# Layer one of a hybrid decoder: input products by seven quarter sums, with the recurrence fed from DRAM

## The chip, the cores and the metric

One core of a Trainium2 chip runs the whole program. The metric is the device time of one execution in microseconds (us), and the change is judged by the median of several executions of the kernel before and after it. The engines are PE (TensorE: matmuls and transposes), DVE (VectorE), ACT (ScalarE), POOL (GpSimd) and SP, the queue from which every DMA of this kernel is issued.

## The reference

The program is a decoder trunk of two layers over x of 1024 tokens by 1024 features. Layer one is a gated linear recurrence (HGRN2) with 16 heads of 128; layer two is forgetting attention (FoX) with keys and values of its own. The change is in layer one:

```python
q, fz, i, g = jnp.split(h @ w_in, 4, axis=-1)      # h: 1024 x 1024, w_in: 1024 x 8192
logf = jnp.log(lb + (1.0 - lb) * jax.nn.sigmoid(fz))
k = (1.0 - lb) * jax.nn.sigmoid(-fz)
...
b = jnp.cumsum(logf, axis=3)                        # within chunks of 64 tokens
q_dec, k_in, k_st = q * jnp.exp(b), k * jnp.exp(-b), k * jnp.exp(b_last - b)
att = jnp.where(causal, jnp.einsum('bhnck,bhnsk->bhncs', q_dec, k_in), 0.0)
...                                                 # state = dl * state + k_st^T v, o = q_dec state + att v
o = _rms(o, onorm_g.reshape(A_HEADS, HEAD_DIM))
return (o * jax.nn.silu(g)) @ w_out
```

## The kernel before

Every large product is made in three passes: each operand is split into a high part that the PE takes fast and a low remainder (`halves`: a copy on ACT, then a subtraction on POOL or DVE), and high*high, high*low and low*high are summed in PSUM. The activations h, transposed and split, stay in SBUF.

Layer one works through eight pairs of heads (`hg_pair`). A pair takes four weight matrices of 1024 by 256 columns, here called v, g, f and q after what they make (value, gate, forget, query). g, f and q are made transposed (`gemm_T`, head dimension in the partitions, 512 tokens in a row: 24 matmuls of 512 columns for a head and token half); v is made with tokens in the partitions (`gemm_N`, 192 matmuls of 256 columns). One such matrix is the unit of time of this document; a pair is four of them.

Around the products runs the recurrence, for both heads of a pair and one half of the tokens at a time (`hg_half`). Its pieces for one head and half are: `hg_forget` (three sigmoid and logarithm passes on ACT, a scan and a chain of small operations on DVE, four exponentials on ACT, products on DVE; each switch between sigmoid, logarithm and exponential loads a table), `hg_att` (8 matmuls, a masked copy on DVE, 4 transposes), `hg_state` (up to 4 matmuls and a chain of DVE steps), `hg_out` (8 matmuls, then a square on ACT and on DVE the reduction L542, the helper `rsqrt_mean` with 12 operations of 128x4, and the product L544) and `hg_turn` (4 transposes, a scaled copy on ACT, a product with the gate on POOL, stores to DRAM). Beside these, three column pairs of the condition's projections are summed on DVE in every pair (`mod_sum`, L268 and L271: eight operations for each).

The order on PE is fixed while the program is written: a class `Weave` chains all PE instructions, and the pieces of the recurrence are generators that are advanced after so many microseconds of product work (`yield 4.5` and the like). The order on DVE, ACT, POOL and SP is the scheduler's. Each engine works its own list strictly in that order.

## Time and profile before

| | us |
|---|---|
| median of 3 runs (2373.2 to 2376.35) | 2374.51 |
| the profiled execution, own time | 2370.9 |
| its span, first to last instruction | 2369.2 |
| one pair in the steady part (158.9 to 271.8) | 112.9 |
| PE busy in it | 109.3 |
| DVE, ACT, POOL busy in it | 66.9, 49.4, 27.0 |

The profile is of one execution. The second group of the table is read from a stretch that holds one pair exactly; PE's busy time counts matmuls that overlap in its pipeline, so what matters is where it stands idle and how far apart equal instructions start.

### The profile page before, as it was taken

To read this page: it belongs to the slowest core of one execution; us is meant where nothing else is said; L and a number is where in the kernel's file an instruction comes from. 1 tells how busy PE (TensorE), PEld (TensorE's weight loads), DVE (VectorE), ACT (ScalarE), POOL (GpSimd) and SP (SyncE) were. 2 spreads that over 40 slices of the span, in tenths; PEclk is the share of its full clock that TensorE was granted. 3 is DMA by queue.
4 is the path that set the end of the run, shared out by engine and by line. 5 is a ranking of instruction groups with operands and counts; after the bars stand their busy time and mean duration, and the time that the engine had idled before them with its cause. 6 is when DMAs were issued, how large, how long until landed. Compare 5 with 4: busy or idle time off the path is not lost.

```text
span 2369.2 us, 38021 instructions
## 1 busy us (share of the span) xinstructions
PE 2263.2 (96%) x14376; PEld 2026.4 (86%) x14376; DVE 1501.3 (63%) x3838; ACT 1016.6 (43%) x1634; POOL 601.9 (25%) x514
## 2 busy tenths in 40 slices
PE   4999999999999999999798999999999999999999
PEld 3888888888888798788688999989999999998887
DVE  7565555665656566646867547667767766777533
ACT  5454444444353536324323324444544544455321
POOL 3222222221222221101332222433343334333000
PEclk9999999999999999999899999999999999999999
DMA  8313131313132223565322323512222222235443
GB/s 272 102 41 103 45 98 46 98 54 98 55 89 72 72 85 95 189 217 182 106 90 81 124 86 99 177 57 68 88 74 73 88 78 84 68 94 175 154 145 115
DMA packets 220315, 245.18 MB, mean 103 GB/s; under 512 B 14610, under 2 KB 182964, under 8 KB 220132
## 3 DMA queue, kind: packets, MB, share of 16 engines
q1 hardware_dynamic: 220132, 242.75, 32.8%
q8 instruction: 113, 1.85, 0.3%
q14 instruction: 70, 0.57, 0.1%
HBM read 196.36 MB, written 46.34 MB: 102 GB/s over the span
## 4 chain that ended last, share of the span: by engine, by line
PE 73%; DVE 11%; ACT 6%; issue 4%; DMA 4%; POOL 1%; SPq 0%; ACTq 0%; DVEq 0%; POOLq 0%
PE mm L48 53%; PE oa L48 8%; PE sm L48 7%; PE sm L51 5%; DVE blk L233 2%; DVE blk L271 1%; DVE dl L479 1%; ACT blk L232 1%; DVE blk L473 1%; ACT L472 1%; DMA blk<-in_mod_w_dram 1%; ACT L487 1%; ACT blk L472 1%; POOL blk L233 1%; ACT L470 1%
## 5 line engine op out<-in xcount | busy, mean ns | idle before, releaser
L48 PE MATMUL mm<-blk,blk 128*128 128x512 f32 (+1 forms) x9120 | 1726.0, 343 | 15.2 <-DVE blk L233 7.9
L48 PEld LDWEIGHTS mm<-blk,blk 128*128 128x128 f32 x9120 | 1419.5, 192 | 185.9 <-DVE blk L233 10.5
L232 ACT ACTIVATE blk<-blk 128x1024 fp32r<-128x1024 f32 (+3 forms) x372 | 335.4, 914 | 461.2 <-PE mm L48 281.1
L233 DVE TENSOR_TENSOR blk<-blk,blk 128x1024 fp32r<-128x1024 f32 (+3 forms) x268 | 276.2, 1039 | 228.8 <-ACT blk L232 225.2
L233 POOL TENSOR_TENSOR blk<-blk,blk 128x1024 fp32r<-128x1024 f32 (+1 forms) x104 | 240.0, 2314 | 308.6 <-ACT blk L232 302.5
L48 PE MATMUL oa<-blk,blk 128*128 128x256 f32 (+1 forms) x2016 | 286.4, 287 | 27.8 <-DVE blk L523 14.7
L48 PEld LDWEIGHTS oa<-blk,blk 128*128 128x128 f32 x2016 | 267.4, 196 | 39.2 <-DVE blk L523 16.0
L48 PE MATMUL sm<-blk,blk 128*128 128x256 f32 (+6 forms) x1824 | 269.2, 303 | 0.1
L48 PEld LDWEIGHTS sm<-blk,blk 128*128 128x128 f32 (+2 forms) x1824 | 218.2, 175 | 23.2 <-issue 3.5
L51 PE MATMUL sm<-ident,blk 128*128 128x128 f32 x1201 | 187.8, 277 | 36.2 <-DVE blk L931 12.6
L51 PEld LDWEIGHTS sm<-ident,blk 128*128 128x128 f32 x1201 | 144.6, 142 | 63.3 <-issue 32.0
L1226 ACT ACTIVATE blk<-blk,m 128x128 f32<-128x128 f32 (+7 forms) x128 | 99.0, 773 | 127.5 <-DVE m L1224 117.4
L233 DVE TENSOR_TENSOR blk<-sm,blk 128x512 fp32r<-128x512 f32 (+1 forms) x160 | 92.9, 581 | 62.7 <-ACT blk L232 62.2
L1228 POOL TENSOR_SCALAR blk<-blk,smx 128x128 f32<-128x128 f32 (+7 forms) x128 | 98.1, 767 | 135.6 <-DVE smx L1227 121.2
L271 DVE SCALAR_TENSOR_TENSOR blk<-blk,cc,blk 128x256 f32<-128x256 f32 x196 | 111.2, 570 | 20.6 <-DMA blk<-in_mod_w_dram 13.8
L1198 POOL TENSOR_TENSOR blk<-rows4k,keep 128x128 f32<-128x128 f32 x128 | 63.0, 492 | 226.8 <-DVE mx L1205 208.4
L553 POOL TENSOR_TENSOR blk<-blk,blk 128x512 f32<-128x512 f32 x32 | 42.5, 1327 | 238.4 <-ACT blk L552 238.4
L232 ACT ACTIVATE blk<-sm 128x512 fp32r<-128x512 f32 (+1 forms) x160 | 81.1, 507 | 48.7 <-PE sm L51 47.9
L1205 DVE CUSTOM_DVE_ANT_0 blk<-sm,rows4k 128x128 f32<-128x128 f32 (+3 forms) x176 | 84.6, 494 | 22.9 <-PE sm L48 21.4
L474 POOL TENSOR_SCALAR blk<-blk,cc 128x512 f32<-128x512 f32 x32 | 22.9, 716 | 260.7 <-ACT blk L471 257.4
L487 ACT ACT_TABLE_LOAD x31 | 39.8, 1283 | 103.0 <-DVE blk L482 103.0
L473 DVE TENSOR_TENSOR_SCAN blk<-rows4k,blk 128x512 f32<-128x512 f32 x32 | 39.1, 1223 | 70.3 <-ACT blk L472 70.3
(167 smaller groups left out, 1776.2 us busy)
## 6 DMA issues: line engine op xcount, KB each, us to landing
blk<-in_a_w_in_dram SPq DMA_DIRECT2D x64, 512.0 KB, 3.9
blk<-in_mod_w_dram SPq DMA_DIRECT2D x48, 512.0 KB, 4.7
blk<-in_kv_w_dram SPq DMA_DIRECT2D x32, 512.0 KB, 4.1
blk<-in_b_w_in_dram SPq DMA_DIRECT2D x32, 512.0 KB, 3.9
ogd<-blk SPq DMA_DIRECT2D x128, 64.0 KB, 1.9
blk<-in_kv_mod_w_dram SPq DMA_DIRECT2D x16, 512.0 KB, 3.5
blk<-in_a_w_out_dram SPq DMA_DIRECT2D x16, 512.0 KB, 3.9
blk<-ogd SPq DMA_DIRECT2D x16, 512.0 KB, 3.8
```

What stands on the lines that cost most here:

```text
L48: self._chain(self.PE.matmul(*a, **k))
L51: self._chain(self.PE.transpose(*a, **k))
L232: S.activation(hi, src, AF.Copy)
L233: eng.tensor_tensor(lo, src, hi.bitcast(F32), ALU.subtract)
L271: V.scalar_tensor_tensor(acc, rawk(rb, k), csil[:, k:k + 1], acc, ALU.mult, ALU.add)
L472: S.activation(u["lf"], u["lf"], AF.Ln, bias=lc, scale=oc)
L473: V.tensor_tensor_scan(u["b"], rst, u["lf"], 0.0, ALU.mult, ALU.add)
L487: S.activation(lf[:, :, 1, :], lf[:, :, 1, :], AF.Exp)
L1198: G.tensor_tensor(nfm, nF[:, i * P:n], negm, ALU.add)
L1205: V.tensor_tensor_reduce(dst, src, add, 1.0, -3e38, ALU.add, ALU.max, mx[:, nm:nm + 1])
L1226: S.activation(l[:, 0:n], l[:, 0:n], AF.Exp, bias=m, accum_out=sm)
L1228: G.tensor_scalar(l[:, 0:n], l[:, 0:n], sm, 0.0, ALU.mult, ALU.add)
```

## The change

From the second kind of the first pair on, each weight matrix (29 of 32; v, f and q of the first pair stay as they were) is multiplied by the scheme of seven products of quarters: activations and weights are cut in two along both the contraction and the other dimension, seven sums or differences of quarters are made on each side, seven products of 512 x 128 x 512 are made instead of eight, and the four quarters of the result are put together from them. The seven operands of the activations are made once (`sums`). Those of the weights are made matrix by matrix (`sa_prep`): four sums and differences on POOL, seven splits with the low part on POOL for five of them and on DVE for two. A product of a quarter is 12 matmuls of 512 columns; `sa_step` names them m = 1, 6, 2, 7, 5, 4, 3, in this order, in three PSUM banks. A result is read by ACT or added up by DVE (L747 to L757) and stored to DRAM, 256 KB for a head and token half.

The recurrence becomes a thread for each head and token half (`hg_thread`), four a pair, started after 19.0 units of product work each (the program counts 28 ticks of 0.68 for a matrix). A thread loads its f, q and v from DRAM, and g later; v arrives transposed and is turned with 4 transposes more (`hg_values`). Two threads have a set of buffers each; a third waits for the turn of the first. The condition's sums are now one for each matrix, for the first 24 matrices.

```diff
-    def hg_half(p, th, v, sg):
-        for j in range(2):
-            hg_att(j)
-            PE.marks.add(("att", p, j, th))
-            yield 4.5
...
-        for j in range(2):
-            hg_out(2 * p + j, j, th, v)
-            PE.marks.add(("out", p, j, th))
-            yield 5.0
-        yield 2.0
-        for j in range(2):
-            hg_turn(2 * p + j, j, th, sg)
-            yield 3.0
...
+    def hg_thread(p, i):
...
+        if i >= 2 or p > 0:
+            yield from PE.wait(("turn", *((p, i - 2) if i >= 2 else (p - 1, i + 2))))
+        hg_load(p, i)
+        yield 3.5
+        if not first:
+            yield from PE.wait(("gate", *before))
+        hg_forget(p, i, None if first else 1 - j)
+        PE.marks.add(("forget", p, i))
+        yield 10.0
+        hg_att(j)
+        yield 3.0
+        hg_values(j)
+        yield from PE.wait(("mat", "g", p, i))
+        dma(us[j]["g"], hgd["g", p, i])
+        PE.marks.add(("gate", p, i))
+        yield 2.5
+        hg_state(j, th)
+        yield 5.0
+        hg_out(j, th)
+        yield 6.0
+        if not last:
+            yield from PE.wait(("forget", *((p, i + 1) if i < 3 else (p + 1, 0))))
+        hg_turn(p, i)
+        PE.marks.add(("turn", p, i))
+        yield 0.0
...
+    def hg_spawn(p):
+        for i in range(4):
+            PE.spawn(hg_thread(p, i), (2.0 + 19.0 * i) if p + 1 < NP else (2.0, 15.0, 33.0, 46.0)[i])
...
+        b11, b12, b21, b22 = B(0, 0), B(0, 1), B(1, 0), B(1, 1)
+        if m == 6:
+            G.tensor_tensor(b12, b22, b12, ALU.subtract)
+            G.tensor_tensor(b11, b11, b12, ALU.add)
+        if m == 7:
+            G.tensor_tensor(b21, b21, b11, ALU.subtract)
+        if m == 5:
+            G.tensor_tensor(b11, b22, b11, ALU.subtract)
+        halves(V if m in (6, 5) else G, *sa_slot(i), {1: b11, 6: b11, 2: b21, 7: b12, 5: b11, 4: b21, 3: b22}[m])
...
+        for k in range(4):
+            ah, al = [c512(full(m, k // 2, lo).bitcast(F32R))[:, k % 2, :] for lo in range(2)]
+            for y, (lh, rh) in enumerate(((wh, ah), (wh, al), (wl, ah))):
+                PE.matmul(ps, lhsT=lh[:, k, :], rhs=rh, start=first and k == 0 and y == 0,
+                          stop=last and k == 3 and y == 2, skip_group_check=True)
+            PE.tick(0.68)
...
+        if xi == 5 and n < len(mods_left):
+            acc = accs[n % 2]
+            mod_sum((raw_next(), acc))
+            PE.spawn(mod_later(mods_left[n], acc), 8.0)
+        sa_prep(i + 2)
+        sa_step(i)
```

On POOL, in the steady part of layer one, a whole pair of the kernel before stands in these rows and the few before them: splits of weights 1024 wide (L233), the scale of k (L474), the product with the gate (L553).

```order
L474 TENSOR_SCALAR blk_1_106<-blk_1_106,cc 128x512
L233 TENSOR_TENSOR blk_1_88<-blk_1_96,blk_1_86 128x1024
L233 TENSOR_TENSOR blk_0_91<-blk_0_93,blk_0_89 128x1024
L233 TENSOR_TENSOR blk_1_92<-blk_1_94,blk_1_90 128x1024
L553 TENSOR_TENSOR blk_0_117<-blk_0_117,blk_0_99 128x512
L553 TENSOR_TENSOR blk_0_117<-blk_0_117,blk_1_100 128x512
```

In the kernel after, the following rows are less than one matrix of the four. L237 are low parts (of the operands m = 2, 7, 4, 3 and of the next matrix's 1), L727, L724, L729 and L725 the sums of weight quarters, L508 the scale of k, L597 the product with the gate.

```order
L237 TENSOR_TENSOR blk_1_1034<-blk_1_106,blk_1_1034 128x512
L727 TENSOR_TENSOR blk_1_106<-blk_1_106,blk_0_105 128x4x128
L724 TENSOR_TENSOR blk_0_93<-blk_1_94,blk_0_93 128x4x128
L729 TENSOR_TENSOR blk_0_105<-blk_1_106,blk_0_105 128x4x128
L508 TENSOR_SCALAR blk_0_813<-blk_0_813,cc 128x512
L237 TENSOR_TENSOR blk_0_1035<-blk_0_105,blk_0_1035 128x512
L237 TENSOR_TENSOR blk_1_1034<-blk_1_106,blk_1_1034 128x512
L237 TENSOR_TENSOR blk_0_1035<-blk_1_106,blk_0_1035 128x512
L597 TENSOR_TENSOR blk_0_817<-blk_0_817,blk_1_820 128x512
L237 TENSOR_TENSOR blk_0_1033<-blk_0_95,blk_0_1033 128x512
L725 TENSOR_TENSOR blk_0_95<-blk_0_95 128x4x128
```

What moved: between the low parts of m = 2 and m = 7 stand three sums and the scale of k in one run, and there are 12 POOL operations a matrix where there were four.

On DVE, the normalisation of one thread's result stands behind the forget chain of the next. Before, the rows from the last products of a forget chain (L489, L488, L490) to the reduction of a result (L542) are these, with state steps (L525, L520) and the product with q (L633) between them.

```order
L489 TENSOR_TENSOR blk_1_110<-blk_1_106,blk_0_105 128x4x64
L525 SCALAR_TENSOR_TENSOR blk_1_116<-blk_1_116,dl,sm 128x128 x2
L633 TENSOR_TENSOR blk_0_111<-mm,blk_1_108 128x512
L525 SCALAR_TENSOR_TENSOR blk_1_116<-blk_1_116,dl,sm 128x128
L488 TENSOR_TENSOR blk_0_109<-blk_0_109,blk_1_106 128x512
L520 TENSOR_SCALAR blk_1_116<-blk_1_116,dl 128x128
L490 TENSOR_TENSOR blk_1_110<-blk_0_109,dl 128x4x64
L542 TENSOR_REDUCE ss<-blk_1_112 128x4
```

After, L749 adds up the result of m = 6, L523, L522 and L525 are the products of the forget chain, L237 is the low part of the operand of m = 5, L582 the reduction, and the rows of 128x4 behind it the start of `rsqrt_mean`.

```order
L749 TENSOR_TENSOR blk_0_115<-mm,blk_0_115 128x512
L561 TENSOR_SCALAR blk_0_821<-blk_0_821,dl 128x128
L523 TENSOR_TENSOR blk_1_818<-blk_1_818,blk_0_817 128x512
L522 TENSOR_TENSOR blk_0_819<-blk_0_819,blk_1_818 128x512
L525 TENSOR_TENSOR blk_0_819<-blk_1_818,dl 128x4x64
L237 TENSOR_TENSOR blk_0_1035<-blk_0_93,blk_0_1035 128x512
L582 TENSOR_REDUCE ss<-blk_1_814 128x4
L225 TENSOR_SCALAR rs_m<-ss 128x4
L226 TENSOR_SCALAR rs_t<-rs_m 128x4
L227 TENSOR_SCALAR rs_y<-rs_t 128x4
```

What moved: the low part of a PE operand is now in this list, and in every matrix the normalisation of a result, for which PE waits, begins behind the whole forget chain of another head.

On PE, the transposes of `hg_turn` (L51, x4) wait for that normalisation. Before, 33 matmuls of 512 columns stand between the last of `hg_out` and the first turn, whose end is this:

```order
L48 MATMUL mm<-blk_0_73,blk_1_90 128x512
L48 MATMUL mm<-blk_1_74,blk_1_90 128x512
L48 MATMUL mm<-blk_0_73,blk_1_92 128x512
L51 MATMUL sm<-ident,blk_1_112 128x128 x4
L48 MATMUL mm<-blk_0_75,blk_1_90 128x512
L48 MATMUL mm<-blk_1_76,blk_1_90 128x512
```

After, the turn stands in the last quarter of the step m = 5 (its weights are in block 1035), and 24 matmuls lie between `hg_out` and it; the row behind the three that follow begins m = 4.

```order
L48 MATMUL mm<-blk_1_826,blk_0_1035 128x512
L48 MATMUL mm<-blk_0_825,blk_0_1035 128x512
L51 MATMUL sm<-ident,blk_1_814 128x128 x4
L48 MATMUL mm<-blk_0_825,blk_0_1035 128x512
L48 MATMUL mm<-blk_1_826,blk_0_1035 128x512
L48 MATMUL mm<-blk_0_825,blk_0_1035 128x512
L48 MATMUL mm<-blk_0_89,blk_0_1033 128x512
```

What moved: the turn comes after fewer matmuls, and what follows it (m = 4, `hg_att`, m = 3, `hg_values`) is queued behind it.

## Rows read from the trace of the kernel before

**Rows 1.** Windows of one pair: window, length, busy us (count) by engine, clock, DMA.

```profile
158.90:271.80 112.90, 109.33 (x673) 95.45 (x672) 66.92 (x157) 49.37 (x68) 26.96 (x17) 0.98 0.25 75
```

**Rows 2.** Chain that ended last: first products of pairs 1 and 7 (start, us, what).

```profile
158.94 5.74 PE mm L48 x48
...
838.14 5.74 PE mm L48 x48
```

**Rows 3.** The same chain within a pair, 271 to 385 us.

```profile
279.18 4.31 PE mm L48 x36
...
288.77 0.44 PE sm L51 x4
...
317.72 25.19 PE mm L48 x111
...
348.14 5.50 PE mm L48 x24
...
354.56 1.02 PE sm L48 x12
...
376.88 6.18 PE mm L48 x24
```

**Rows 4.** Groups by shape, 264 to 377 us: count, busy us, mean ns, idle before.

```profile
L233 POOL TENSOR_TENSOR blk<-blk,blk 128x1024 fp32r<-128x1024 f32 x8 | 19.0, 2380 | 27.4 <-ACT blk L232 27.4
...
L271 DVE SCALAR_TENSOR_TENSOR blk<-blk,cc,blk 128x256 f32<-128x256 f32 x21 | 11.6, 552 | 1.3 <-DMA blk<-in_kv_mod_w_dram 0.9
...
L553 POOL TENSOR_TENSOR blk<-blk,blk 128x512 f32<-128x512 f32 x4 | 5.5, 1370 | 25.7 <-ACT blk L552 25.7
```

**Rows 5.** Timeline of DVE (start, us): small operations, alone and beside POOL.

```profile
301.85 2.38 DVE L227 SCALAR_TENSOR_TENSOR rs_y<-rs_t,rs_y 128x4 f32<-128x4 f32 x1
...
336.94 0.17 DVE L479 COPY dl<-blk 128x4 f32<-128x4 f32 x1
...
360.70 2.19 DVE L479 COPY dl<-blk 128x4 f32<-128x4 f32 x1
```

**Rows 6.** Timeline of POOL at the same places.

```profile
301.82 4.72 POOL L233 TENSOR_TENSOR blk<-blk,blk 128x1024 fp32r<-128x1024 f32 x2 [10.52 <-ACT blk L232]
...
360.50 2.36 POOL L233 TENSOR_TENSOR blk<-blk,blk 128x1024 fp32r<-128x1024 f32 x1 [2.42 <-ACT blk L232]
```

**Rows 7.** Timeline of ACT in one forget chain.

```profile
332.06 0.60 ACT L470 ACTIVATE blk<-mm 128x512 f32<-128x512 f32 x1 [4.12 <-PE mm L48]
...
334.46 0.82 ACT L472 ACTIVATE blk<-blk,cc 128x512 f32<-128x512 f32 x1
337.78 1.28 ACT L487 ACT_TABLE_LOAD   x1 [2.50 <-DVE blk L482]
...
340.02 0.61 ACT L486 ACTIVATE blk<-blk 128x512 f32<-128x512 f32 x1
```

**Rows 8.** Timeline of DVE in the same chain.

```profile
335.69 1.22 DVE L473 TENSOR_TENSOR_SCAN blk<-rows4k,blk 128x512 f32<-128x512 f32 x1
...
337.27 0.42 DVE L482 TENSOR_TENSOR blk<-dl,blk 128x256 f32<-128x256 f32 x1
...
340.66 0.69 DVE L488 TENSOR_TENSOR blk<-blk,blk 128x512 f32<-128x512 f32 x1 [0.64 <-ACT blk L486]
341.39 0.42 DVE L490 TENSOR_TENSOR blk<-blk,dl 128x256 f32<-128x256 f32 x1
```

**Rows 9.** Timeline of DVE: two normalisations, first and last operation of each.

```profile
276.50 0.68 DVE L542 TENSOR_REDUCE ss<-blk 128x4 f32<-128x512 f32 x1
...
279.60 0.69 DVE L544 TENSOR_TENSOR blk<-oa,rs_y 128x512 f32<-128x512 f32 x1
...
308.51 0.68 DVE L542 TENSOR_REDUCE ss<-blk 128x4 f32<-128x512 f32 x1
...
313.97 0.68 DVE L544 TENSOR_TENSOR blk<-oa,rs_y 128x512 f32<-128x512 f32 x1
```

**Rows 10.** DMA issues: KB each, median us from issue to landing.

```profile
vd<-blk SPq DMA_DIRECT2D x32, 256.0 KB, 2.9
```

More of the change, by code (lines that the diff above doesn't have):

```diff
@@ L60, in _step, with wait @@
             self.threads.remove(th)
+    def wait(self, mark):
+        while mark not in self.marks:
+            yield 0.5
     def tick(self, us):
@@ L186, in hybrid_trunk_kernel @@
     V.memset(st1, 0.0)
-    xt = [ar(14 + t // 2, (t % 2) * 1024, 1024) for t in range(NT)]
+    xt = [ar(t // 2, (t % 2) * 1024, 1024) for t in range(NT)]
     def load_x(*ts):
@@ new lines, in hg_thread @@
+    def hg_thread(p, i):
+        j, th = i % 2, i // 2
+        first, last = (p, i) == (0, 0), (p, i) == (NP - 1, 3)
+        before = (p, i - 1) if i else (p - 1, 3)
+        if i >= 2 or p > 0:
[23 more added lines that the diff above has]
+        yield 0.0
@@ L641, in mod_later, with put, early @@
         yield 0.0
-    for p in range(NP):
-        wv, wg = hg_pair(p, wv, wg)
+    stage = [ar(20, 0, 512), ar(20, 512, 512), ar(24, 1024, 512), ar(24, 1536, 512)]
+    def put(kind, p, i, ps, to, eng=S):
+        if eng is S:
+            S.activation(to, ps, AF.Copy)
+        else:
+            V.tensor_copy(to, ps)
+        dma(hgd[kind, p, i], to)
+    def early(kind, w, i, to):
+        ps = mm_ps()
+        gemm_T(ps, w, i % 2, i // 2)
+        put(kind, 0, i, ps, to, V if i % 2 else S)
@@ new lines, in hybrid_trunk_kernel, with full, sums, whole @@
+    renew(16, 17)
+    wv = split_a((16, 17))
+    for i in range(4):
+        put("f", 0, i, fps[i], stage[i], V if i % 2 else S)
+    for i in range(2):
+        put("q", 0, i, qps[i], us[i]["b"], V if i % 2 else S)
+    for i in (2, 3):
+        early("q", wq, i, us[i - 2]["ks"])
+    for j in range(2):
+        G.memset(us[j]["att"], 0.0)
+    def full(m, kk, lo, n=1024):
+        return pr(AOPS0[m][kk], 1024 * lo, n)
+    def sums(kk):
+        x, y, w = [pr(b, 1024 * kk, 1024) for b in (19, 23, 18)]
+        z = (pr(20, 0, 1024), pr(24, 1024, 1024))[kk]
+        def whole(eng, dst, m):
+            eng.tensor_tensor(dst, full(m, kk, 0), full(m, kk, 1), ALU.add)
+        whole(G, y, 4)
+        whole(V, z, 1)
+        whole(V, x, 3)
+        whole(G, w, 2)
+        V.tensor_tensor(y, y, x, ALU.add)
+        V.tensor_tensor(x, z, x, ALU.subtract)
+        V.tensor_tensor(z, y, z, ALU.subtract)
+        V.tensor_tensor(w, w, z, ALU.subtract)
+        def split(m, src):
+            halves(V, full(m, kk, 0).bitcast(F32R), full(m, kk, 1).bitcast(F32R), src)
+        split(7, x)
+        split(6, z)
+        return [lambda: split(5, y), lambda: split(3, w)]
@@ new lines, in hybrid_trunk_kernel @@
+    rst = ar(24, 1536, 512)
+    G.memset(rst, 1.0)
+    G.memset(c64(rst)[:, :, 0:1], 0.0)
+    renew(19, (20, (0,)))
+    hg_spawn(0)
+    sa_prep(0)
+    sa_prep(1)
+    for part in later:
+        part()
+    for i, (n, m) in enumerate(SSTEPS):
+        xi = i - 7 * n
+        if xi == 0:
+            for _ in range(2 if n < len(mods_left) else 1):
+                raw_load()
+        if xi == 5 and n < len(mods_left):
[4 more added lines that the diff above has]
+        sa_step(i)
+        if xi == 6 and MATS[n][0] == "q":
+            hg_spawn(MATS[n][1])
@@ L647, in gate_rows @@
+    hblk[:] = range(8)
     def gate_rows(l, gt, row):
@@ L823, in a_ready @@
     def a_ready(t):
-        PE.need(("half", NP - 1, t // 4))
+        for j in range(2):
+            PE.need(("turn", NP - 1, 2 * (t // 4) + j), fair=True)
     def a_row(t, ch):
```

243 lines of the change are left out of this document (124 added, 119 removed).

## The prediction

> **What bounds the kernel now.** First the windows of one pair of layer one [rows 1]: PE is busy for 109.3 of 112.9 us, DVE for 66.9, POOL for 27.0. So PE sets the time here, with 3.6 us of idle. Then the chain that ended last: the first products of pair 1 and pair 7 start at 158.94 and 838.14 us [rows 2], so a pair takes (838.14 - 158.94) / 6 = 113.2 us, and a matrix, a quarter of it, **28.3 us**. That is the figure against which the change has to be set. The chain within a pair [rows 3] is PE nearly throughout: 111 matmuls of 512 columns take 25.19 us, 0.227 each; 36 of 256 columns take 4.31, 0.120 each; four transposes 0.44. Last, who makes PE wait: the groups of POOL [rows 4] and the timelines of DVE and POOL side by side [rows 5, 6]. A copy of 128x4 on DVE takes 0.17 us at 336.94 and 2.19 at 360.70; in between nothing differs but a POOL subtraction that runs from 360.50 to 362.86, and the copy ends 0.03 us behind it. A rsqrt step at 301.85 takes 2.38 us beside the first of two such subtractions. These operations of DVE do not run beside a POOL operation; they end with it.
>
> **What the products save.** A matrix falls from 96 matmuls of 512 columns to 84: 12 x 0.227 = 2.7 us. The v matrix, 192 x 0.120 = 23.0 us before, was 1.2 us more than 96 x 0.227 = 21.8, or 0.3 a matrix; v's transposes in every thread cost 0.44. PE's work of a matrix was 109.3 / 4 = 27.3, and becomes 27.3 - 2.7 - 0.3 + 0.4 = **24.7 us**. If PE were never kept waiting, 28 matrices would give back 28 x 3.6 = 101 us. So the question is what else becomes the bound.
>
> **What the other engines get.** POOL had 27.0 / 4 = 6.7 us a matrix. Now it has five low parts, four sums, two gate products, each of 512 elements, and the scale of k: the 1024-wide one takes 2.38, the 512-wide ones up to 1.37, a lone one about 1.3 [rows 4], so 11 x 1.3 plus at most 1.3 makes about 15.0. DVE had 16.7 and gets two low parts, five additions of results and, for 24 matrices, one condition sum where it had three quarters of one; it loses the product that made the gate. That is about 6 us more, 22 to 23 of 28.3. Neither is full by itself, but DVE works its list in order, waits for POOL operation by operation, and PE waits for DVE in each matrix: for the low part of the operand of m = 5, then for the normalised result that `hg_turn` transposes.
>
> **The loop that sets a matrix.** I follow one matrix from the end of `hg_values` to the same point in the next; each leg is queued behind the one before it.
>
> - ACT to the logarithm. The copy of v and one high part lie ahead (0.5 each by the spacing of the ACT rows), then two sigmoids, the table and the logarithm: 332.06 to 335.28 is 3.2 us [rows 7]. Together 4.2.
> - DVE, scan to the subtraction for which the exponentials wait: 335.69 to 337.69, 2.0 us when POOL is idle [rows 8]. But here POOL has the low part for m = 2, three sums, the scale of k and the low part for m = 7 in one run, six operations, some 7.4 us that begin with the ACT leg. The scan gets in between two of them (1.2 us) and each small copy behind it waits for the next, as in rows 5; so the subtraction ends about 7.4 + 1.2 + 0.7 = 9.3 us after the start of the loop, not 6.2. I take 9.3 for the two legs.
> - ACT, table and four exponentials: 337.78 to 340.63, 2.9 us [rows 7].
> - DVE: the product with q (0.6), the two k products (340.66 to 341.81, 1.15 [rows 8]), the low part for m = 5 (0.6), and one low part of POOL (m = 4) in their way, 1.3: 3.6. Alone 2.3; with two operations in the way 4.9.
> - DVE, normalisation: 276.50 to 280.29, 3.8 us alone, 308.51 to 314.65, 6.1 us with a condition sum's pieces in between [rows 9]. In three orders of four the list after has such pieces there, and POOL's low part for m = 3 falls into it. I take 5.0 for the 24 matrices with a condition sum and 4.2 for the others.
> - PE, from the turn to the end of `hg_values`: 0.4, three matmuls of m = 5 (0.7), m = 4 (2.7), `hg_att` with its transposes (1.5), m = 3 (2.7), 0.4: 8.4 us [rows 3].
>
> The sum is 9.3 + 2.9 + 3.6 + 5.0 + 8.4 = 29.2, and some 0.1 us at each of five hand-overs: **29.7 us** with a condition sum, **28.9** without. PE's own work of 24.7 lies inside it: PE would stand idle for about 5 us of each matrix, most of it in m = 5 and at the turn, since only 24 matmuls (5.5 us) cover the way from `hg_out` to the turn.
>
> **The sum.** 24 x (29.7 - 28.3) = 33.6 and 4 x (28.9 - 28.3) = 2.4. The first pair: before, 2.5 matrices of 21.8 us after the start-up, 54.5; after, six products of 24 matmuls (32.7) and one matrix in seven parts (19.1), 51.8, behind which the quarter sums of the activations must come in time: taken as even. The last threads run into the output projection, as the last half pair did, but two of them are started after the last matrix: +4, between 0 and 10. Results of 256 KB go to DRAM and come back: a store like it lands in 2.9 us [rows 10], a load takes no less, and the slices lie a matrix ahead of their reading except v's and g's of the first thread, which lie some 10 us ahead. I cost this at nothing; cover gone, it is the third rival. Added to the profiled execution's own 2370.9 this makes 2410.9; the runs' median lies 3.6 above that execution, so the forecast in their terms is **2414 us**.
>
> **A rule of the skill.** The rows show DVE operations with two operands in SBUF, and a copy, ending together with POOL's [rows 5, 6]. The Trainium skill, page "SBUF — State Buffer", section "Who interferes with whom", says that a DVE instruction with two SBUF inputs, or in a two-port mode, and a GpSimd instruction that reads SBUF exclude each other for the whole instruction, and that the one issued first wins. By that rule the trace agrees. It speaks against this change, and by it alone a matrix could not take less than the two engines' excluding work together, which the first rival prices from rows.
>
> **The rivals.**
>
> *The lists interleave better than my loop has it; faster.* It is so if POOL's run of six is mostly done before the scan, so that the second leg falls back to 6.2 and the others to 2.9, 2.3, 3.8, 8.4 and 0.5: 24.1, below PE's 24.7. Then what excludes each other is left: POOL's 15.0, and of DVE eight steps of the condition sum at 0.5 (the mean of 0.55 has waits in it [rows 4]), the scan 1.2, copies and subtractions 1.3, the k and q products 2.2, two low parts 1.3, the rsqrt steps 2.3, about 12: 27.0 with a condition sum and 23 without, where PE's 24.7 binds. That gives 2370.9 + 24 x (27.0 - 28.3) + 4 x (24.7 - 28.3) + 4 = 2329, in the runs' terms 2333; if even the excluding work is hidden, 28 x 3.6 = 101 less, 2278. For it: PE loses only 3.6 us a pair now, with lists of the same scheduler. Against it: no two lists have stood this full beside each other, and a 128x4 copy already waits 2 us for each POOL operation that it meets.
>
> *DVE is full; slower still.* The condition sum's steps after the turn meet the gate product, the low part of the next m = 1, a sum and the gate's product (5.2 us of POOL), the addition that frees the bank of m = 3 is queued behind them, and PE's first matmuls after each wait are slower, as 24 matmuls took 6.18 us after a wait against 5.50 [rows 3]: 2.3 us more a matrix, 32.0. 2370.9 + 24 x 3.7 + 4 x 1.5 + 4 = 2470, or 2473. It decides from a DVE of some 28 us a matrix on.
>
> *DRAM is not hidden; slower.* SP issues in order; a store that waits for POOL's gate product holds back the load of a slice or of the weights behind it. With 2.9 us for a store and as much for a load once in each matrix beyond its cover, some 2 us a matrix: 2370.9 + 28 x 3.3 + 4, about 2467. For it: SP's list has stores and loads mixed. Against: weights are fetched two matrices ahead.
>
> *Nothing to see:* gain and wait cancel to within 0.2%, about what a measurement of this kernel can tell from no change.
>
> **Chances and range.** The loop as worked out 0.40, better interleaving 0.36, DVE full 0.13, DRAM 0.05, within 0.2% 0.06. Slower are the first, third and fourth, less 0.02 for the loop's lower edge, which I give to the first rival: slower 0.56, the same 0.06, faster 0.38. The loop's own range, by its bounds of 3.6 (2.3 to 4.9) and 5.0 (3.8 to 6.2), is 2384 to 2450. For eight in ten I need all but the far end of the first rival and the worst of the second: **2315 to 2468**.
>
> **What would show it.** Right: PE's idle time in layer one named after DVE's normalisation (before the transposes of the turn) and after the low part of a weight operand, 4 to 6 us a matrix; 84 matmuls of 512 columns a matrix still at 0.227; DVE's rsqrt steps and small copies with means well above 0.17; POOL 14 to 16 us a matrix; start-to-start of matrices 29 to 30.5 us. Wrong: matrices 25 to 28 us apart with no wait at the turn (first rival), idle PE named after additions of results, with DVE busy throughout (second), or idle PE, ACT or POOL named after a DMA (third). If scan and copies turn out not to wait for POOL's run, the second leg is 3 us too long, and that alone turns the sign.

## The result and the profile after

The kernel after takes 2483.22 us (median of 4 runs, 2482.53 to 2485.37), the kernel before 2373.86 in the same comparison: ratio 1.0462, 95% interval 1.0444 to 1.048. It is slower, as forecast, but by 109 us and not by 40, and 2483 lies outside the range.

The profiled execution of after took 2485.37 us (span 2483.7), 114.5 more than that of before. The page's first part and the clock row of its second:

```profile
PE 2235.5 (90%) x13384; PEld 1952.4 (79%) x13384; DVE 1695.4 (68%) x4032; ACT 1118.3 (45%) x1850; POOL 885.5 (36%) x755
...
PEclk9999898999999999989989999999999999999999
```

PE has 13384 matmuls and transposes (14376 before), and the granted clock has eights among the nines. How far apart matrices are is read from ACT, which copies the first result of each (L747); the second pair of rows is the copy of v (L549), where the prediction's loop begins, in two neighbours. Timeline of ACT:

```profile
160.55 0.60 ACT L747 ACTIVATE blk<-mm 128x512 f32<-128x512 f32 x1 [0.48 <-DMA hg<-blk]
...
502.35 0.60 ACT L549 ACTIVATE blk<-sm 128x512 f32<-128x512 f32 x1
505.27 0.63 ACT L500 ACTIVATE blk<-blk 128x512 f32<-128x512 f32 x1 [2.33 <-DMA blk<-hf]
...
536.33 0.58 ACT L549 ACTIVATE blk<-sm 128x512 f32<-128x512 f32 x1
...
1001.04 0.58 ACT L747 ACTIVATE blk<-mm 128x512 f32<-128x512 f32 x1
```

From the 2nd matrix to the 29th it is (1001.04 - 160.55) / 27 = **31.13 us** a matrix, where [rows 2] gave 28.3; the one shown takes 33.98. In it ACT stands 2.33 us until its f has landed from DRAM (L500); in 270 to 900 us it does so 11 times, 15.1 us in all. What PE waits for, 270 to 1000 us (total us, times, longest):

```profile
PE sm L51 <- DVE blk L584: 100.8, 24, 6.5
PE mm L48 <- ACT blk L519: 5.5, 6, 1.7
PE mm L48 <- DVE blk L749: 2.9, 5, 0.7
```

One wait, once in each of 24 matrices, 4.2 us each: the transposes of `hg_turn` wait for the normalised result (L584). The chain that ended last, through the matrix from 502.35 (start, us, what), answers to [rows 3]:

```profile
508.88 0.82 ACT blk L504
...
510.95 1.15 DVE blk L507
...
512.45 0.44 DVE blk L516
512.96 1.28 ACT L521
...
516.68 0.34 DVE blk L525
517.01 0.59 DVE ss L582
517.61 1.33 DVE blk L272
518.94 1.14 DVE rs_m L225
...
521.58 0.60 DVE blk L754
...
523.66 0.70 DVE blk L584
524.50 1.08 PE sm L51 x4
525.58 4.77 PE mm L48 x12
...
531.96 3.45 PE mm L48 x15
535.41 0.44 PE sm L51 x4
```

Behind that load it is the loop of the prediction, leg by leg: logarithm, scan and subtraction (L507 to L516), table and exponentials (L521), products (L525), normalisation (L582 to L584), then PE from the turn to the copy of v. The 12 products behind the turn take 4.77 us; at the 0.227 of [rows 3] they would take 2.72. The windows of all matrices, and of the next turn before, during and behind its wait, show why (length, busy us (count) of PE, PEld, DVE, ACT, POOL, granted clock, DMA):

```profile
160.55:1001.04 840.49, 717.19 (x3665) 583.28 (x3664) 607.90 (x1217) 412.99 (x642) 426.29 (x324) 0.92 0.44 138
547.30:553.00 5.70, 5.68 (x24) 4.43 (x24) 4.36 (x11) 2.88 (x6) 2.81 (x2) 1.00 0.63 221
553.00:558.20 5.20, 0.06 (x1) 0.00 (x0) 4.96 (x14) 0.50 (x1) 2.73 (x2) 0.90 0.60 199
558.20:563.20 5.00, 4.94 (x15) 3.64 (x17) 3.44 (x5) 1.97 (x2) 1.28 (x1) 0.50 0.26 91
```

The clock is 1.00 over the 24 products, and 0.50, the 1.2 GHz level, for 5 us behind the wait. A matrix keeps PE busy for 717.19 / 27 = 26.6 us, DVE for 22.5, POOL for 15.8. The normalisation that this wait is for, on DVE (start, us; in brackets idle before):

```profile
549.32 0.68 DVE L582 TENSOR_REDUCE ss<-blk 128x4 f32<-128x512 f32 x1
550.03 0.55 DVE L225 TENSOR_SCALAR rs_m<-ss 128x4 f32<-128x4 f32 x1
551.88 0.47 DVE L272 TENSOR_SCALAR blk<-blk,cc 128x256 f32<-128x256 f32 x1 [1.31 <-DMA blk<-in_mod_w_dram]
...
552.39 0.49 DVE L275 SCALAR_TENSOR_TENSOR blk<-blk,cc,blk 128x256 f32<-128x256 f32 x1
...
553.84 1.22 DVE L230 TENSOR_TENSOR rs_t<-rs_t,rs_m 128x4 f32<-128x4 f32 x1
...
555.17 0.69 DVE L754 TENSOR_TENSOR blk<-mm,blk 128x512 f32<-128x512 f32 x1
...
557.42 0.69 DVE L584 TENSOR_TENSOR blk<-oa,rs_y 128x512 f32<-128x512 f32 x1
```

Where [rows 9] show 3.8 us alone, this is 8.8: a wait of 1.31 for a condition weight, four steps of the sum, a 128x4 product stretched to 1.22 by POOL, and a result's addition (L754) all stand in DVE's list ahead of L584.

**The ledger**, in profiled terms, with the transposes that open the output projection (PE L51, `sm<-ident,cc`) as the mark; they start at 945.60 in before and at 1028.48 after. The 28 matrices: 28 x (31.13 - 28.3) = +79.2 (forecast +36). The first pair: 1028.48 - 28 x 31.13 = 156.8 against 158.94, -2.1 (forecast even). The end: in before the mark lies 5.7 us ahead of the last pair's end (158.94 + 7 x 113.2 = 951.3), and from the mark to PE's last instruction it is 1449.8 us after and 1418.6 before, +31.2; together +36.9 (forecast +4). The sum is 114.0 of the 114.5.

### The profile page after: what moved, and what is told of

Read it like the earlier page. It is cut to its first block, busy times and chain, and to the rows that moved or that the text cites. A ratio compares the mean times of both kernels' runs of the same rounds, so it can differ in the third digit from the quotient of the medians.

```text
span 2483.7 us, 37625 instructions
## 1 busy us (share of the span) xinstructions
PE 2235.5 (90%) x13384; PEld 1952.4 (79%) x13384; DVE 1695.4 (68%) x4032; ACT 1118.3 (45%) x1850; POOL 885.5 (36%) x755
## 3 DMA queue, kind: packets, MB, share of 16 engines
q8 instruction: 106, 1.74, 0.3%
## 4 chain that ended last, share of the span: by engine, by line
PE 64%; DVE 20%; DMA 5%; issue 5%; ACT 5%; POOL 1%; SPq 0%; DVEq 0%; ACTq 0%; POOLq 0%
PE mm L48 43%; PE sm L48 7%; PE oa L48 7%; PE sm L51 6%; DVE blk L275 2%; DVE blk L237 2%; DVE rs_t L230 1%; DVE rs_t L229 1%; DMA blk<-hf 1%; DVE blk L507 1%; DVE rows4k L275 1%; ACT blk L236 1%; DVE blk L584 1%; DVE rs_y L231 1%; ACT L521 1%
## 5 line engine op out<-in xcount | busy, mean ns | idle before, releaser
L48 PE MATMUL mm<-blk,blk 128*128 128x512 f32 (+1 forms) x8028 | 1691.9, 362 | 29.5 <-DVE blk L237 7.3
L48 PEld LDWEIGHTS mm<-blk,blk 128*128 128x128 f32 x8028 | 1327.3, 195 | 227.1 <-DVE blk L237 10.6
L236 ACT ACTIVATE blk<-blk 128x512 fp32r<-128x512 f32 (+3 forms) x525 | 409.9, 790 | 519.8 <-PE mm L48 329.4
L237 DVE TENSOR_TENSOR blk<-blk,blk 128x1024 fp32r<-128x1024 f32 (+3 forms) x334 | 329.4, 992 | 233.3 <-ACT blk L236 230.8
L237 POOL TENSOR_TENSOR blk<-blk,blk 128x512 fp32r<-128x512 f32 (+1 forms) x191 | 307.8, 1616 | 357.2 <-ACT blk L236 352.8
L51 PE MATMUL sm<-ident,blk 128*128 128x128 f32 x1329 | 218.5, 288 | 175.9 <-DVE blk L584 138.3
L51 PEld LDWEIGHTS sm<-ident,blk 128*128 128x128 f32 x1329 | 165.1, 147 | 216.5 <-issue 183.9
L48 PE MATMUL oa<-blk,blk 128*128 128x256 f32 (+1 forms) x2016 | 275.6, 282 | 3.5 <-ACT blk L1080 3.2
L48 PE MATMUL sm<-blk,blk 128*128 128x256 f32 (+6 forms) x1800 | 273.2, 308 | 0.1
L48 PEld LDWEIGHTS oa<-blk,blk 128*128 128x128 f32 x2016 | 260.7, 192 | 12.7 <-ACT blk L1080 3.4
L48 PEld LDWEIGHTS sm<-blk,blk 128*128 128x128 f32 (+2 forms) x1800 | 220.8, 177 | 31.5 <-issue 13.6
L275 DVE SCALAR_TENSOR_TENSOR blk<-blk,cc,blk 128x256 f32<-128x256 f32 x196 | 146.5, 749 | 12.6 <-DMA blk<-in_mod_w_dram 5.5
L1338 POOL TENSOR_TENSOR blk<-rows4k,keep 128x128 f32<-128x128 f32 x128 | 62.7, 490 | 228.1 <-DVE mx L1345 208.9
L237 DVE TENSOR_TENSOR blk<-sm,blk 128x512 fp32r<-128x512 f32 (+1 forms) x160 | 93.0, 581 | 62.4 <-ACT blk L236 61.9
L597 POOL TENSOR_TENSOR blk<-blk,blk 128x512 f32<-128x512 f32 x32 | 42.7, 1334 | 168.5 <-ACT blk L596 168.5
L596 ACT ACTIVATE blk<-sm,cc 128x512 f32<-128x512 f32 x32 | 22.0, 687 | 172.6 <-PE sm L51 172.6
L757 DVE TENSOR_TENSOR blk<-mm,blk 128x512 f32<-128x512 f32 x87 | 60.0, 690 | 51.1 <-PE mm L48 49.0
```

Of the source, the lines that this page charges most:

```text
L48: self._chain(self.PE.matmul(*a, **k))
L51: self._chain(self.PE.transpose(*a, **k))
L236: S.activation(hi, src, AF.Copy)
L237: eng.tensor_tensor(lo, src, hi.bitcast(F32), ALU.subtract)
L275: V.scalar_tensor_tensor(acc, rawk(rb, k), csil[:, k:k + 1], acc, ALU.mult, ALU.add)
L597: G.tensor_tensor(u["ogT"], u["ogT"], u["g"], ALU.mult)
```

## The experiments

All edits are against the kernel after. "Spacing" is that of its matrices, "clock" the granted clock of 270 to 900 us, "end" the us from the transposes that open the projection to the same row of PE counted from the program's end, the 8751st (before: 56.3). Ratios are to the kernel before. e3, e7, e11 and e18 leave work out, and e9 and e10 use wrong weights, so these six are bounds and not candidates.

| run | us | ratio (95%) | spacing | clock | end |
|---|---|---|---|---|---|
| after | 2483.22 | 1.0462 (1.0444 to 1.048) | 31.13 | 0.92 | 81.6 |
| e1_turn_later | 2464.91 | 1.0394 (1.0378 to 1.041) | 30.00 | 0.94 | 91.7 |
| e2_fill_wait | 2523.66 | 1.0636 (1.061 to 1.0663) | 32.13 | 0.96 | 96.2 |
| e3_no_sums | 2447.29 | 1.0319 (1.0303 to 1.0334) | 29.77 | 0.94 | 82.9 |
| e4_early_slices | 2441.9 | 1.0291 (1.0269 to 1.0313) | 29.32 | 0.95 | 79.1 |
| e5_turn_later_early | 2494.71 | 1.0517 (1.0501 to 1.0532) | 31.55 | 0.92 | 85.1 |
| e6_out_later_early | 2429.04 | 1.0241 (1.0219 to 1.0264) | 29.03 | 0.96 | 80.7 |
| e7_no_pool_sums | 2453.0 | 1.0338 (1.032 to 1.0357) | 29.85 | 0.94 | 81.0 |
| e8_out_later | 2526.96 | 1.0648 (1.0632 to 1.0664) | 32.31 | 0.90 | 91.7 |
| e9_sums_later | 2408.0 | 1.0149 (1.0134 to 1.0164) | 28.16 | 0.97 | 80.9 |
| e10_gate_on_dve | 2429.75 | 1.0224 (1.019 to 1.0257) | 29.17 | 0.97 | 80.4 |
| e11_later_no_sums | 2369.14 | 0.9982 (0.9972 to 0.9991) | 26.94 | 0.99 | 80.9 |
| e12_last_threads_closer | 2481.88 | 1.0459 (1.0444 to 1.0475) | 31.04 | 0.91 | 81.0 |
| e13_last_pair_side_by_side | 2475.71 | 1.0429 (1.0411 to 1.0446) | 31.08 | 0.92 | 77.5 |
| e14_sums_later | 2428.88 | 1.0232 (1.0217 to 1.0247) | 29.13 | 0.96 | 81.2 |
| e15_both | 2432.67 | 1.0248 (1.0233 to 1.0264) | 29.42 | 0.94 | 79.2 |
| e16_weights_from_pool | 2480.6 | 1.0455 (1.044 to 1.0471) | 30.92 | 0.93 | 81.2 |
| e17_weights_from_act | 2446.37 | 1.0311 (1.0294 to 1.0329) | 29.93 | 0.94 | 81.2 |
| e18_two_last_threads | 2459.87 | 1.0377 (1.0359 to 1.0394) | 31.03 | 0.92 | 62.7 |

### Can the wait at the turn be covered?

Theory: the loop through DVE sets the matrix, and PE waits for the normalisation because too few products cover it. Rival: whatever PE piece is moved, DVE's list holds the next thing that PE needs.

```diff
         hg_out(j, th)
-        yield 6.0
+        yield 9.5
```

> The turn of a thread is issued 3.5 units (12 products) later, behind the attention scores of the next thread. My theory: a matrix takes 31.1 us because PE stands at the turn (4.2 us in each of 24) until a normalisation that DVE does behind the next thread's forget step, and runs at a lower granted clock behind that wait (about 2 us). Then with the turn out of the way the scores no longer wait for the normalisation: matrices 26 to 28.5 us apart, 75 to 140 us less, 2345 to 2410. Rival, DVE is full: the next instruction of PE that needs DVE waits instead, 2470 to 2495. Rival, the DRAM round trip: the slices are fetched 3 us later, 2483 to 2520.

The turn's wait shrinks, and a new one is there. Waits of PE, 270 to 1000 us:

```profile
PE mm L48 <- DVE blk L754: 90.3, 24, 6.4
PE sm L51 <- DVE blk L584: 14.3, 7, 3.8
```

L754 adds a result and so frees a bank of PSUM; in DVE's list it now stands behind the next head's forget chain. 18 us are gained of 100: the matrices give 28 x 1.13 = 32 us, and the end, 91.7 us in place of 81.6, takes 10 back. Moving `hg_out` instead, alone:

```diff
         hg_state(j, th)
-        yield 5.0
+        yield 8.5
```

> Output and turn 3.5 units later, slices fetched after the turn as in the kernel after, and so 3 us later than there. My theory: the place of the output in DVE's list does most of it, 2390 to 2430. Rival, the DRAM round trip: the gate logits of a thread land too late for its forget step, ACT's sigmoids are named after a transfer in every matrix, 2460 to 2500.

It loses 44 us. In 270 to 900 us POOL waits 135.7 us for the weights' DMA (2.2 in after), ACT 25.3 for f's load (15.1), PE still 56.8 at the turn, and 42.5 more named after the rsqrt steps L229 to L231. e1 is for the rival. e8 is for it in part: PE still waits for DVE, but why the weights come so much later there is not traced. In both, an order that suits all engines would have to be found for all pieces together.

Next the wait was filled with 12 products whose result is not used, ahead of the turn's transposes, to keep PE busy and so to price the clock:

```diff
         pg = sm_ps()
+        for n in range(12):
+            PE.matmul(pg, lhsT=pr(14, 0, 128, F32R), rhs=pr(14, 0, 512, F32R), start=True, stop=True)
```

> Twelve products of 512 columns whose result is overwritten are put ahead of the turn's transposes, 2.7 us at 0.227 each, less than the shortest wait there (3.0). No other instruction changes. If the lower granted clock behind the wait is what lengthened PE's leg from 8.4 to 10.9 us: idle time 4.5 to 1.8 us, clock 0.92 to 0.95 or more, the leg 9 us, matrices 29.3 us apart, 2420 to 2450. If the leg is long for another reason (DVE, POOL or ACT in it), 2475 to 2495.

Timeline of PE at one turn (the L48 row with `sm<-blk` is the filling):

```profile
765.05 2.88 PE L48 MATMUL sm<-blk 128*128 128x512 f32 x12
768.13 0.63 PE L51 MATMUL sm<-ident,blk 128*128 128x128 f32 x4 [0.19 <-DVE blk L584]
768.51 2.99 PE L48 MATMUL mm<-blk,blk 128*128 128x512 f32 x12
...
775.95 3.01 PE L48 MATMUL mm<-blk,blk 128*128 128x512 f32 x12 [2.14 <-DVE blk L759]
```

The 12 products behind the turn take 2.99 us here and not 4.77. But the scheduler has put the other engines' lists in another order, new waits stand elsewhere (17.8 us for the addition L759, L757 in after), and the kernel is 40 us slower, outside both ranges. Nor does the leg from the turn to the copy of v fall to 9 us: with the new waits in it, it takes 11.1 us on the mean (10.9 in after). As a price of the clock this run is inconclusive; e3 gives it.

### What loads DVE and POOL

```diff
-            mod_sum((raw_next(), acc))
+            V.tensor_scalar(acc, rawk(raw_next(), 0), csil[:, 0:1], None, ALU.mult)
```

> Left out: seven of the eight steps of each condition sum within layer one's matrices (the scale and gate of later layers come out wrong); their transfers stay. My theory: every matrix is like the ones without a sum, 29.2 us against a mean of 31.1, so 28 x 1.9 = 53 less, 2420 to 2445. Rival, DVE is full: 4 us of DVE a matrix go, and a matrix falls by most of that, 2370 to 2400. Rival, the DRAM round trip: 2470 to 2485.

With one step of each condition sum left of eight, 36 us are gained; PE still waits 92.1 us at the turn. Over the 23 matrices the normalisation takes 6.6 us as before (6.7), so the seven steps alone are not what made it long: the sum's first step still waits for its weight there (1.51 us at 526.13), and POOL and L754 are met as before. The run also holds two matrices alike in their work and in the wait, but not in the clock. Windows from one copy of v to the next:

```profile
425.21:452.18 26.97, 24.59 (x137) 20.27 (x136) 17.81 (x42) 15.53 (x25) 13.87 (x11) 1.00 0.46 146
543.07:571.62 28.55, 26.17 (x137) 21.39 (x136) 17.66 (x42) 15.53 (x26) 13.96 (x11) 0.94 0.47 155
```

And the timeline of PE at their turns:

```profile
443.27 0.63 PE L51 MATMUL sm<-ident,blk 128*128 128x128 f32 x4 [2.38 <-DVE blk L584]
443.65 3.01 PE L48 MATMUL mm<-blk,blk 128*128 128x512 f32 x12
...
561.12 0.63 PE L51 MATMUL sm<-ident,blk 128*128 128x128 f32 x4 [2.38 <-DVE blk L584]
561.51 4.58 PE L48 MATMUL mm<-blk,blk 128*128 128x512 f32 x12
```

The same 137 matmuls, the same wait of 2.38 us; PE is busy for 24.59 us at a clock of 1.00 and for 26.17 at 0.94. The clock's price is 1.6 us of such a matrix.

POOL's four sums for a matrix left out:

```diff
-        if m == 6:
-            G.tensor_tensor(b12, b22, b12, ALU.subtract)
-            G.tensor_tensor(b11, b11, b12, ALU.add)
-        if m == 7:
-            G.tensor_tensor(b21, b21, b11, ALU.subtract)
-        if m == 5:
-            G.tensor_tensor(b11, b22, b11, ALU.subtract)
```

> Left out of the kernel after: the four sums of weights that POOL makes for each matrix (the products then use raw quarters). If they matter by standing in the way of the scan and of the small copies behind it: the leg from the logarithm to the subtraction falls from 4.7 us to 2 to 3, a matrix by 1.5 to 2.5, 2415 to 2445. If DVE and POOL excluding each other is itself the bound: 5.2 us a matrix less, 2340 to 2370. If POOL's work is no part of it: 2475 to 2490.

30 us are gained, and from the start of the logarithm to the end of the subtraction it takes 3.9 us, not 4.7, so POOL's run does hold DVE up there. PE still waits 94.6 us at the turn. Neither load by itself is the bound.

### DRAM: slots and queues

`ogT`, from which the finished head is stored, shares a buffer with `lf`, into which the next thread loads f. Here it shares one with `kst`, and the load waits only for `hg_out`:

```diff
-        return dict(lf=lf, k=k, b=b, eb=b, ks=ks, kst=kst, qd=qd, sq=b, kT=k, v=v, g=g, ogT=lf,
+        return dict(lf=lf, k=k, b=b, eb=b, ks=ks, kst=kst, qd=qd, sq=b, kT=k, v=v, g=g, ogT=kst,
...
-            yield from PE.wait(("turn", *((p, i - 2) if i >= 2 else (p - 1, i + 2))))
+            yield from PE.wait(("out", *((p, i - 2) if i >= 2 else (p - 1, i + 2))))
...
         hg_out(j, th)
+        PE.marks.add(("out", p, i))
```

> The gated result takes the place of the decayed k instead of the gate logits, and a thread's slices are fetched once the thread two before has made its output, not its turn: no load waits for the store of a result any more. My theory: the loop stays, only the leg to the logarithm falls from 3.9 us towards 2.4 in the matrices where it was long, and the end of layer one loses its idle stretch of 12.6 us at 1061: 2440 to 2468. Rival, the DRAM round trip is in each matrix: 1.5 x 28 = 42 and the end's 15 to 20, 2420 to 2430. If the transfers are hidden anyway: only the end, 2463 to 2470.

41 us are gained: more than the 15.1 us that ACT waits for f in 630 us of after, since DVE's order changes as well: the forget chain is now done ahead of the output, and DVE waits for ACT's square before the reduction L582 (40.5 us, 21 times in 270 to 900), which in after stood directly behind the chain. How much of the 41 us is the wait and how much the order is not separated. With e1's edit added:

> The turn 3.5 units later and the early slices together. My theory by now: what holds PE is DVE's list, in which the addition that frees the bank of m = 4 stands behind the normalisation or the next forget step; here it still stands behind the normalisation, so PE's wait is named after that addition, 2 to 3 us a matrix, matrices 28.5 to 30 us apart, 2430 to 2460. If the two gains add up (18 and 41 less): 2424 or less.

Not additive: PE now waits 96.9 us (23 times) for the copy of v. With e8's edit in its place:

> The output of a thread, and with it the turn, 3.5 units later, and the early slices. In DVE's list the addition of m = 7 now stands ahead of the normalisation, and 27 products and the scores of the next thread lie between output and turn. My theory: PE waits for less than 2 us a matrix, its clock stays above 0.97, matrices 26 to 27.5 us apart, 2350 to 2400. Rival, DVE is full (26 us of it busy in each matrix of the run with early slices, waits for POOL among them): matrices 28.5 to 30 us apart, 2430 to 2460, with PE's wait named after additions or low parts.

The turn's wait falls to 21.3 us in 270 to 900, and 21.4 more stand at the copy of v. The spacing, 29.03, is the rival's, but PE's waits are not named after additions or low parts. DVE waits for weights now; its waits there:

```profile
DVE blk L272 <- DMA blk<-in_mod_w_dram: 49.8, 12, 4.7
DVE blk L272 <- DMA blk<-in_kv_mod_w_dram: 24.1, 6, 4.5
```

Four runs asked whether these 74 us are the condition weights' loads or the place of the sums. First e6 with the sums one product later (`if xi == 5` becomes `if xi == 6`); by a slip each sum there takes the weights loaded for the next matrix's products, and these the sum's, so that its numbers come out wrong:

> As the run with output later and early slices, and the condition sum of a matrix one product block later in the program. There DVE stood 74 us (18 times, 2.5 us a matrix) at the first step of a sum, whose weights had not landed, with everything PE wants behind it. My theory: most of that wait goes, matrices 26.5 to 28 us apart, 2350 to 2400. If DVE is full anyway and the wait only filled idle time: 2415 to 2435.

DVE's waits for weights are gone and 21 us with them. One more run, e10, changes e9 again: DVE multiplies the turned result by the gate itself, in place of ACT's scaled copy and POOL's product. If DVE and POOL getting in each other's way was what is left, 15 to 30 us less were expected; if DVE's own load was, 20 more. It takes 22 us more (2429.75, one of four runs 2415.84), and PE waits 39.0 us (17 times) for DVE's addition L749, which is for DVE's own load. Now the later sums with their own weights:

```diff
         if xi == 5 and n < len(mods_left):
-            acc = accs[n % 2]
-            mod_sum((raw_next(), acc))
-            PE.spawn(mod_later(mods_left[n], acc), 8.0)
+            todo = (raw_next(), accs[n % 2])
+        if xi == 6 and n < len(mods_left):
+            mod_sum(todo)
+            PE.spawn(mod_later(mods_left[n], todo[1]), 8.0)
```

> Output later, early slices, and the condition sums one product block later, with their own weights (in the run before with sums later the sum and the next matrix had taken each other's weights). DVE's waits for those weights fall from 74 us to under 30, matrices 28 to 28.5 us apart, 2398 to 2414. If the wait only moves: 2422 to 2435.

It equals e6, and DVE waits 50.3 and 23.7 us as there: the scheduler leaves DVE's list nearly as it was in e6, with the sum where its weights are late. Then e6 with all weights' loads of layer one issued from POOL's list, and from ACT's (`nc.scalar`):

```diff
-                dma(ar(b, 1024 * q, 1024).rearrange("p (k n) -> p k n", n=256),
+                raws["q"](ar(b, 1024 * q, 1024).rearrange("p (k n) -> p k n", n=256),
...
+    raws["q"] = nc.gpsimd.dma_start
     hg_spawn(0)
```

> As the run with output later and early slices; the weights of layer one's matrices and sums are fetched by instructions in POOL's list, not in SP's, where they stood behind stores and slice loads that wait for other engines. If SP's order is what made the condition weights late there (DVE stood 74 us at them): the wait goes and the matrices fall from 29.0 to 26.5 to 28 us, 2355 to 2405. If the weights are late since their buffer comes free late, or POOL's issuing costs as much: 2415 to 2450.

> The same with the weights fetched from ACT's list. If SP's order is it: 2355 to 2405. If ACT's list waits in its turn for the buffer to come free, with the copies and exponentials behind it: 2430 to 2480.

From POOL DVE's wait grows to 62.3 + 33.2 us, and POOL waits 109.6 us (35 times) for the buffer that DVE's last step L275 frees. In e6 itself SP stands at the loads of weights (L248) until earlier readers of their buffer are done; the waits of SP, 270 to 900:

```profile
SPq L248 <- DVE blk L237: 58.9, 21, 5.2
SPq L248 <- DVE blk L275: 41.8, 26, 4.5
```

So the loads are late because their buffer comes free late: SP reaches them before that. From ACT, DVE waits only 8.9 + 15.1 + 5.9 us, but PE waits 66.3 at the turn again; why DVE waits less there is not traced. Both lose against e6.

Last, e6 with e3's edit:

> As the run with output later and early slices; left out: seven of the eight steps of each condition sum in layer one's matrices. Bound of what the sums cost there: 4 us of DVE work and 2.5 us of waits in each of 24 matrices. My theory: PE becomes the bound, 25 to 26 us a matrix, 2315 to 2350. If something else holds (ACT's 17 us, POOL): 27.5 or more, 2385 or more.

```profile
270.00:900.00 630.00, 588.62 (x3170) 475.44 (x3169) 482.07 (x920) 396.69 (x588) 378.70 (x280) 0.99 0.49 160
```

Only with the sums out and the order changed is PE nearly full (idle 41.4 of 630 us, clock 0.99, 26.94 a matrix), and even that version, which leaves work out, is 0.2% ahead of before, because its end is as long as that of after: 28 x (26.94 - 28.3) = -38 us in the matrices, +37 at the end.

### The end of layer one

The last threads' start, in units of product work:

```diff
-            PE.spawn(hg_thread(p, i), (2.0 + 19.0 * i) if p + 1 < NP else (2.0, 15.0, 33.0, 46.0)[i])
+            PE.spawn(hg_thread(p, i), (2.0 + 19.0 * i) if p + 1 < NP else (2.0, 12.0, 22.0, 32.0)[i])
```

> The kernel after, with the last pair's four threads started at 2, 12, 22 and 32 units in place of 2, 15, 33 and 46 (the last one 9.5 us of products earlier). The 82 us between the last matrix and a fixed product of the output projection (57 before) are, by my theory, a chain from thread to thread (turn, store, load, forget step, normalisation, turn): no change, 2475 to 2490. If the start times set it: 8 to 10 us less, 2472 to 2476.

The last pair's threads two and two beside each other, and the same on e14 (there with a second wait for the turn, ahead of the forget step):

```diff
+        own = p + 1 == NP
-        if not first:
+        if not first and (not own or i == 0):
             yield from PE.wait(("gate", *before))
...
-        if not last:
+        if not own:
             yield from PE.wait(("forget", *((p, i + 1) if i < 3 else (p + 1, 0))))
...
-            PE.spawn(hg_thread(p, i), (2.0 + 19.0 * i) if p + 1 < NP else (2.0, 15.0, 33.0, 46.0)[i])
+            PE.spawn(hg_thread(p, i), (2.0 + 19.0 * i) if p + 1 < NP else (2.0, 4.0, 27.0, 29.0)[i])
```

> The kernel after, with the last pair's threads started two by two (2, 4, 27 and 29 units), each taking its own gate's sigmoid at its turn, so that the second head waits neither for the gate of the first nor the first for the forget step of the second. My theory: four of 32 threads are left after the last product, before went through them two heads at a time in 40 us, after one by one in 95; then the 82 us from the last product to a fixed product of the output projection fall by 15 to 27, 2455 to 2468. Rival, that stretch is set by the projection's weights and SP's list: 2475 to 2490.

> The last two together. If the end of layer one and the matrices are apart from each other the gains add up: 2378 to 2398, against 2373 of the kernel before.

None shortens the end by more than 4.1 us. In e13 the third thread's f still waits for the first one's store (1.74 us) and its own load (5.40) through the shared buffer. The run that decides leaves out two of the four threads:

```diff
-        for i in range(4):
+        for i in range(4 if p + 1 < NP else 2):
```

> The last pair's third and fourth thread (the recurrence of its second token half) are left out; what the first two give is stored for both halves, so two heads' second half is not computed. Products and all else stay. If four threads one after the other make the end long, the stretch from the projection's opening transposes to the same later row falls from 81.6 us to 56 to 62, and the median by 20 to 28, to 2455 to 2463. If the projection's own loads and prefix work set it, the stretch stays above 75 and the median falls by less than 8. In both, the matrices ahead of it stay 31.1 us apart.

The row in the table (62.7) shifts a little with the instructions left out. From the opening transposes to a row behind all threads (the 8500th of PE from the end) it is 113.2 us in before, 141.9 after and 119.6 here. The window of after, then that of e18:

```profile
1028.50:1170.40 141.90, 121.01 (x609) 99.38 (x607) 79.22 (x162) 63.80 (x85) 12.81 (x12) 0.94 0.55 173
```

```profile
1025.40:1145.00 119.60, 109.00 (x508) 89.41 (x506) 59.90 (x102) 43.24 (x55) 6.06 (x6) 0.97 0.58 189
```

Two threads carry 22.3 of the 28.7 us: 12.0 are PE's own work on them (121.01 - 109.00, at the clock of each run), which no start time removes, and 10.3 are waits. Most of these stand at the turn of the second thread, whose normalisation DVE has behind the scan of the third. Start times can reach the waits alone, and e12, e13 and e15 reached 4.1 us of them at the most. Timeline of PE at this turn, in after and in e18:

```profile
1074.19 1.09 PE L51 MATMUL sm<-ident,blk 128*128 128x128 f32 x4 [12.61 <-DVE blk L584]
```

```profile
1063.30 1.09 PE L51 MATMUL sm<-ident,blk 128*128 128x128 f32 x4 [4.82 <-DVE blk L584]
```

## Why the prediction was right in sign and wrong in size

**The way it goes: right.** Matrices are spaced by the loop through ACT, DVE and PE. PE waits for the normalisation 24 times in 24 matrices, idle (840.49 - 717.19) / 27 = 4.6 us in each, forecast about 5; POOL 15.8, forecast 15.0; DVE 22.5, forecast 22 to 23; small DVE operations stretched (L225 0.73 us on the mean, L230 0.28, L513 0.53, against 0.17). PE's work of 24.7 was right too, at full clock: 24.59 in e3. Wrong was the second place of the wait: the transposes have it alone, and none of note stands behind a weight operand's low part.

**The legs**, means of 23 matrices, in the order of the loop:

| leg | forecast | measured |
|---|---|---|
| copy of v to the subtraction L516 | 9.3 | 8.6 |
| table, exponentials, products, to the reduction L582 | 2.9 + 3.6 | 4.9 |
| normalisation, L582 to L584 | 5.0 (4.2) | 6.7 |
| turn to the next copy of v, hand-overs | 8.4 + 0.5 | 10.9 |
| sum | 29.7 (28.9) | 31.1 |

The step that failed is the last leg: **I priced "PE, from the turn to the end of `hg_values`" at 8.4 us, from rows in which PE had not waited.** At full clock it is right (9.06 with its hand-over at 443 us of e3), but behind the wait that the same loop forecasts PE gets a granted clock of 0.50 (558 to 563 us above). I had slower matmuls after a wait in the second rival only, from 6.18 against 5.50 in [rows 3], and priced them for a full DVE, though the loop as worked out has the same wait. The price is 1.6 us a matrix in e3, and in after, with longer waits, 26.6 - 24.6 = 2.0 us of PE's busy time. That is as much as the excess of the leg, 10.9 against 8.9, and by itself more than the miss of the matrices, (79.2 - 36) / 28 = 1.5.

The other legs nearly cancel. The normalisation is 1.7 too short, and not for the reason I gave it a higher price (the sum's pieces): e3 leaves seven of eight out and it stays at 6.6. In its place stand the wait for a condition weight, POOL's operations and L754. The first two legs are 0.7 and 1.6 too long: the products behind the exponentials met POOL less often than I took them to (L522 and L523 0.69 us on the mean, what L488 takes alone in [rows 8]). That POOL and DVE exclude each other is seen again; timeline of DVE, beside POOL's subtraction and without it:

```profile
575.97 1.28 DVE L515 TENSOR_TENSOR dl<-blk 128x3 f32<-128x3 f32 x1
...
1035.09 0.15 DVE L515 TENSOR_TENSOR dl<-blk 128x3 f32<-128x3 f32 x1
```

```profile
575.95 1.28 POOL L237 TENSOR_TENSOR blk<-blk,blk 128x512 fp32r<-128x512 f32 x1
```

They start within 0.02 us of each other and end so; L515 takes both its operands from SBUF, and the subtraction reads SBUF. With the rule of the Trainium skill, page "SBUF — State Buffer", section "Who interferes with whom", that I cited ahead, the trace agrees.

**The loop's own range was summed wrong.** Its two bounds taken together, 24 x (1.3 + 1.2) + 4 x 1.3 = 65 us to either side of 2414, give 2349 to 2479; 2384 to 2450 is about what either gives alone. The leg that failed had no bounds at all.

**"+4, between 0 and 10" for the end: wrong**, +36.9. I counted two late threads as the last half pair had been, but four tails stand behind the last matrix, and e18 shows two of them at 22.3 us: work of PE that had lain between products before, and waits at turns with nothing left to cover them. The other 6.4 of the 28.7, the 2.5 behind them and the 5.7 by which before opened its projection ahead of its last pair's end are not traced further.

**The rivals.** Better interleaving: no, though e11 shows that the lists allow 26.9 a matrix without the sums. DVE full: its 2473 is the forecast nearest to the result, but by luck: the end alone gave 33 us that it did not have, and its signs are absent, DVE being busy 22.5 of 31.1 us and PE waiting at the turn. In part it holds: taking work from DVE gains 36 us (e3), adding some costs 22 (e10 against e9), and PE's next operand waits in DVE's list. POOL's load counts as well (30 us, e7). DRAM not hidden: in part; ACT waits 15.1 us for f, I costed the buffers' way through DRAM at nothing, and the shared buffer of `ogT` and `lf` with the order that hangs on it is worth 41 us in e4. How these shares add up stays open: every edit reorders the lists of DVE and ACT, so runs that change two things don't add (e1 -18, e4 -41, both +11).

No version that computes everything beat the kernel before; the best are e6 and e14 with 2429.
